# A norm's factors spread by two products of rounded parts, in place of one product in fp32

## The chip, the cores and the metric

The kernel runs on one core of a Trainium2 chip. The metric is the device time of one execution in microseconds, lower is better. A profiled execution gives, beside its own time, a trace of every instruction on TensorE (PE, with its weight loads listed apart as PEld), VectorE (DVE), ScalarE (ACT), GpSimd (POOL) and SyncE (SP, which only issues transfers here).

## What is computed

A decoder trunk of two layers on 512 tokens of 1024 features. Layer 0 mixes by a causal convolution module, layer 1 by differential attention; each is followed by a SwiGLU feed-forward and a gated embedding. Ahead of each of these parts stands a norm over the features of a token:

```
def rms_norm(x, g):
    xf = x.astype(jnp.float32)
    y = xf * lax.rsqrt(jnp.mean(xf * xf, axis=-1, keepdims=True) + EPS)
    return (y * g.astype(jnp.float32)).astype(x.dtype)

for i in range(DEPTH):                       # DEPTH = 2
    u = rms_norm(h, mixer_norm_g)
    h = h + (conformer_conv(u) if i % 2 == 0 else diff_attention(u))
    u = rms_norm(h, ffn_norm_g[i])
    h = h + swiglu(u, ffn_w_gate[i], ffn_w_up[i], ffn_w_down[i])
    gate = jax.nn.sigmoid(rms_norm(h, ple_norm_g[i]) @ ple_w_gate[i])
    h = h + gate * (p[i] @ ple_w_proj[i])
```

There are six such norms; five of them (all but that ahead of attention) need the factor of a token, the rsqrt, as a row that lies on all 128 partitions.

## The kernel before

**Layout.** The activations lie transposed: eight tiles `h[c]` of 128 features by 512 tokens. A linear layer multiplies weight tiles (128 by 128, stationary) with 512 tokens (moving) and sums over eight feature chunks in PSUM.

**Products in three parts.** Operands are split into a rounded part in the type F32R and the rest, also F32R: `hi` is an ACT copy, `lo = x - hi` a DVE subtraction (for weights lines 159 and 161 in `weight`). `mm3` (lines 164 to 168) adds three products, lo·hi, hi·hi and hi·lo. In the trace both types appear as "f32" on PE; the lines tell them apart. Products of operands that stay in plain fp32 (the sums of columns in line 199, transposes, and line 282 below) are single calls.

**Norms.** The linear layer takes `h * g` without the factor; the factor is multiplied in afterwards, on its result, since it is the same for all features of a token. The way to it:

- `chunk` (or `columns_of_chunks` for the first norm): ACT squares each `h[c]`, POOL adds the squares into `acc`.
- `columns_sum` (line 199): PE sums `acc` over the partitions, in four products of 128 by 128, so that token t of block b stands on partition t.
- `rsqrt_cols`: DVE scales and adds EPS (line 265, 128 by 4 values), POOL raises to -0.5 (line 267). The result `r` is 128 by 4.
- `diagonal` (line 272): DVE multiplies the identity, repeated four times, with `r`: a tile `dg` of 128 by 512 with the factors on four diagonals. It is taken from the four buffers `wk`.
- `spread` (line 282): PE multiplies a matrix of ones with `dg`: every partition of the PSUM tile `tp` then holds the row of 512 factors.
- `rows` (line 257): ACT copies that row to the tile `rb` in SBUF.
- DVE multiplies the accumulators by `rb`: line 514 in the convolution, lines 869 and 871 in the feed-forward, line 912 in the gated embedding.

**Where.** `diagonal` and `spread` are called for five norms: in the convolution's first chunk (lines 496 and 497), in the first pair of each feed-forward (lines 863 and 867) and in each gated embedding (lines 919 and 921). In program order the diagonal stands ahead of one more product of a full chunk (24 calls of 128 by 512), and the spread behind it. The layer norm inside the convolution (lines 575 to 589) builds a diagonal of its own with ACT.

**Order.** The Tile framework's planner writes the order of each engine's instructions: each is given a priority by its place in the program, and the planner, with modelled costs, lets each engine take the first by priority that is ready in its model. On the chip each engine then runs its list in order, so that an instruction that has to wait holds all that stands behind it on the same engine. Some places are tied by hand (`issue_after`, and one stretch with `manual_schedule`). The buffers come from rings under a tag: `wk` has four, `tp` two (PSUM), `mm` four (PSUM), `r8` and `v8` two each.

**Convolution stage.** The eight chunks of the convolution's first layer have their taps run in part on DVE (line 449), in part on ACT and POOL (lines 436, 437), and for four chunks (`PHASED`) on PE (line 398), with a hop through DRAM (`pi`, lines 361 to 367) that lays the tokens out anew; a second hop (`po`) brings the result back.

Of the kernel before, what the change touches and what calls it, by code (L numbers as in the profile page):

```python
# [13 lines left out]
F32R = mybir.dt.float32r  # L14
AF = mybir.ActivationFunctionType
ALU = mybir.AluOpType
# [4 lines left out]
P = 128  # L21
# [70 lines left out]
def trunk(ctx, tc, xT, pT, wts, diag, dww, vec, rel, onehot, lamv, out):  # L92
    nc = tc.nc
    V, A, G, T = nc.vector, nc.scalar, nc.gpsimd, nc.tensor
# [7 lines left out]
    def sb(shape, tag, bufs, dt=F32):  # L102
        uid[0] += 1
        return pool.tile(shape, dt, tag=tag, name=f"{tag}_{uid[0]}", bufs=bufs)
# [8 lines left out]
    wk = lambda dt=F32, shape=(P, S): sb(list(shape), "wk", 4, dt)  # L113
    big = lambda dt=F32, shape=(P, S): sb(list(shape), "big", 5, dt)
    f = lambda ap: ap.bitcast(F32)
# [10 lines left out]
    ident = sb([P, P], "ident", 1)  # L126
    make_identity(nc, ident)
    ones_r = sb([P, P], "ones", 1, F32R)
    ones = f(ones_r)
# [4 lines left out]
    t = wk()[:, 0:P]  # L134
# [4 lines left out]
    t = tp()  # L139
# [69 lines left out]
    class Norm:  # L209
# [41 lines left out]
        def diagonal(self):  # L251
            self.dg = diagonal(self.columns())

        def rows(self):

            r = sb([P, S], "rb", 1)
            A.copy(r, spread(self.dg))
            return r
# [4 lines left out]
    def rsqrt_cols(src, n, inv):  # L263
        v = sb([P, P // 2], "v8", 2)[:, :8]
        last_v[0] = V.tensor_scalar(v[:, :n], src, inv, EPS, ALU.mult, ALU.add)
        r = sb([P, P // 2], "r8", 2)[:, :8]
        last_pow[0] = G.tensor_tensor(r[:, :n], v[:, :n], mhalf[:, :n], ALU.pow)
        return r[:, :n]

    def diagonal(r):  # L270
        dg = wk()
        V.tensor_tensor(
            dg.rearrange("p (b t) -> p b t", b=4),
            ident.unsqueeze(1).to_broadcast([P, 4, P]),
            r.unsqueeze(2).to_broadcast([P, 4, P]),
            ALU.mult,
        )
        return dg

    def spread(dg):  # L280
        t = tp()
        T.matmul(t, ones, dg, start=True, stop=True)
        return t


# [205 lines left out]
    for c in range(NC):  # L491
        wa, wg = pairs[c]
        if c == 0:
            pg = half(wg)
            pa = half(wa)
            norm.dg = diagonal(norm.columns_of_chunks(3))
            rb = norm.rows()
# [81 lines left out]
    r = rsqrt_cols(vs[:, 0:4], 4, 1.0)  # L579
# [4 lines left out]
    dg = wk()  # L584
# [360 lines left out]
    rl = sb([33, NH], "big", 5)  # L945
# [6 lines left out]
    for k in range(2):  # L952
        t = tp()
# [447 lines left out]
```

## Time and profile before

| | before |
|---|---|
| median of 3 runs | 1249.58 us (1247.31 to 1250.39) |
| the profiled execution | 1249.66 us |
| its span, first to last instruction | 1247.6 us |
| granted clock of TensorE | 0.999 |
| ACT busy | 623.0 us (50%) |
| POOL busy | 470.5 us (38%) |
| HBM | 108 GB/s over the span |

How to read the views. A page of the profile gives each engine's busy time and its share of the span. PE's matmuls are pipelined: a matmul of 512 columns is listed with some 0.39 us while the next starts 0.23 us after it, so a busy PE may still be waiting in part; distances between starts, and the chain of waits, say more. The chain of waits is followed back from the last instruction, at each step to what released it, or to the instruction ahead of it on its engine. In the timeline a row gives start and duration in us, engine, line, operation and operands, a count where equal rows were merged, and in brackets the engine's idle time before and what ended it. In the list of waits stand the total, the number and the longest.

### The profile page before, as it was taken

The numbers are of one execution on the slowest core, as the hardware profiler recorded it, in microseconds if no ns is written. First come the engines' busy times: TensorE is split into PE (matmuls) and PEld (weight loads), VectorE is DVE, ScalarE is ACT, GpSimd is POOL, SyncE is SP. The second block draws the span as 40 slices with busy tenths as digits, with TensorE's granted clock in tenths as the row PEclk, the third lists the DMA queues.
The fourth block names the chain that finished last, engine by engine and source line by source line (L and its number), as shares of the span: only waits on it lengthen the run. The fifth ranks groups of instructions, "written<-read, shape, count | busy, mean of one in ns | idle before, by whom it ended". The sixth has DMA issues, their size and how long they took to land.

```text
span 1247.6 us, 18420 instructions
## 1 busy us (share of the span) xinstructions
PE 1236.4 (99%) x7080; PEld 1081.5 (87%) x7080; DVE 877.6 (70%) x1230; ACT 623.0 (50%) x1096; POOL 470.5 (38%) x355
## 2 busy tenths in 40 slices
PE   9999999999999999999999999999999999999998
PEld 7888788888998899888888888788889998999887
DVE  6998866985895478546676876646966885588535
ACT  5653464533553255334666877735434552455432
POOL 3763442024670365132346635041026640562220
PEclk9999999999999999999999999999999999999999
DMA  7566214324233322334432331142333333233321
GB/s 267 175 205 206 82 51 121 96 97 127 85 102 118 102 87 76 109 104 143 122 119 75 113 92 36 51 147 88 92 118 97 102 117 108 82 102 88 104 97 67
DMA packets 49154, 136.33 MB, mean 109 GB/s; under 512 B 5635, under 2 KB 10243, under 8 KB 49068
## 3 DMA queue, kind: packets, MB, share of 16 engines
q1 hardware_dynamic: 46944, 131.74, 33.7%
q10 hardware_dynamic: 2124, 3.43, 1.0%
q8 instruction: 55, 0.90, 0.3%
q14 instruction: 31, 0.25, 0.1%
HBM read 128.84 MB, written 6.31 MB: 108 GB/s over the span
## 4 chain that ended last, share of the span: by engine, by line
PE 88%; DVE 5%; issue 2%; DMA 1%; ACT 1%; SPq 0%; POOL 0%; DVEq 0%; ACTq 0%
PE mm L166 27%; PE mm L167 27%; PE mm L168 27%; PE mm L1117 1%; DVE sc L449 1%; DVE wlo L161 1%; PE sc L1085 1%; PE sc L1084 1%; PE tp L1104 1%; PE sc L398 1%; PE mm L398 1%; PE tp L1038 1%; PE mm L354 1%; PE tp L199 1%; DVE wlo L711 0%
## 5 line engine op out<-in xcount | busy, mean ns | idle before, releaser
L159 ACT CAST whi<-wraw 128x1024 fp32r<-128x1024 f32 (+2 forms) x145 | 145.6, 1013 | 220.2 <-PE mm L168 97.2
L161 DVE TENSOR_TENSOR wlo<-wraw,whi 128x1024 fp32r<-128x1024 f32 (+2 forms) x141 | 179.3, 1277 | 73.7 <-ACT whi L159 73.5
L166 PE MATMUL mm<-A,wlo 128*128 128x512 f32 (+1 forms) x568 | 222.5, 392 | 0.3 <-ACT A L206 0.2
L167 PE MATMUL mm<-A,whi 128*128 128x512 f32 (+1 forms) x568 | 219.8, 388 | 0.0
L168 PE MATMUL mm<-A,whi 128*128 128x512 f32 (+1 forms) x568 | 217.6, 389 | 0.0
L166 PE MATMUL mm<-B,wlo 128*128 128x512 f32 x352 | 137.9, 392 | 0.0
L167 PE MATMUL mm<-B,whi 128*128 128x512 f32 x352 | 137.8, 391 | 0.0
L168 PE MATMUL mm<-B,whi 128*128 128x512 f32 x352 | 136.2, 391 | 0.0
L229 POOL TENSOR_TENSOR acc<-acc,wk 128x512 f32<-128x512 f32 x35 | 58.3, 1665 | 194.5 <-ACT wk L228 193.9
L166 PEld LDWEIGHTS mm<-A,wlo 128*128 128x128 f32 x568 | 106.9, 188 | 23.6 <-issue 1.4
L167 PE MATMUL mm<-C,whi 128*128 128x256 f32 x448 | 127.0, 283 | 0.0
L168 PE MATMUL mm<-C,whi 128*128 128x256 f32 x448 | 127.0, 283 | 0.0
L166 PE MATMUL mm<-C,wlo 128*128 128x256 f32 x448 | 127.0, 283 | 0.0
L167 PEld LDWEIGHTS mm<-A,whi 128*128 128x128 f32 x568 | 107.0, 188 | 22.0 <-issue 1.0
L168 PEld LDWEIGHTS mm<-A,whi 128*128 128x128 f32 x568 | 106.6, 188 | 21.9 <-issue 0.5
L711 DVE TENSOR_TENSOR wlo<-A,whi 128x1024 fp32r<-128x1024 f32 x60 | 104.6, 1752 | 21.0 <-ACT whi L710 21.0
L710 ACT CAST whi<-A 128x1024 fp32r<-128x1024 f32 x60 | 62.9, 1048 | 56.6 <-PE mm L168 45.3
L720 POOL TENSOR_TENSOR A<-wraw 128x512 f32<-128x512 f32 x16 | 25.4, 1589 | 170.3 <-DMA wraw<-in_wts 156.1
L720 POOL TENSOR_TENSOR A<-A 128x512 f32<-128x512 f32 x16 | 25.3, 1581 | 161.9 <-DMA A<-in_wts 159.2
L167 PEld LDWEIGHTS mm<-C,whi 128*128 128x128 f32 x448 | 86.1, 192 | 0.2
L166 PEld LDWEIGHTS mm<-C,wlo 128*128 128x128 f32 x448 | 86.1, 192 | 0.2
L168 PEld LDWEIGHTS mm<-C,whi 128*128 128x128 f32 x448 | 86.1, 192 | 0.0
(309 smaller groups left out, 3030.6 us busy)
## 6 DMA issues: line engine op xcount, KB each, us to landing
wraw<-in_wts SPq DMA_DIRECT2D x161, 512.0 KB, 3.6
A<-in_wts SPq DMA_DIRECT2D x32, 512.0 KB, 3.6
wraw<-in_wts SPq DMA_DIRECT2D x16, 384.0 KB, 3.1
D<-in_diag SPq DMA_DIRECT2D x22, 256.0 KB, 4.7
C<-in_diag SPq DMA_DIRECT2D x16, 256.0 KB, 4.4
h<-in_xT SPq DMA_DIRECT2D x8, 256.0 KB, 5.2
rest<-h SPq DMA_DIRECT2D x8, 256.0 KB, 2.5
bias<-scr ACTq DMA_DIRECT2D x8, 256.0 KB, 3.7
```

The lines of the kernel that those rows point to most:

```text
L159: A.copy(hi[:, cut], raw[:, cut])
L161: eng.tensor_tensor(lo[:, cut], raw[:, cut], f(hi[:, cut]), ALU.subtract)
L166: T.matmul(acc, al, bh, start=first, stop=False, **kw)
L167: T.matmul(acc, ah, bh, start=False, stop=False, **kw)
L168: return T.matmul(acc, ah, bl, start=False, stop=last, **kw)
L199: r = T.matmul(t[:, cut], src[:, cut], ones, start=first and b == 0, stop=last and b == 3)
L229: self.last = self.eng.tensor_tensor(self.acc, self.acc, sq, ALU.add)
L354: last_tap[0] = T.matmul(acc, dg[:, j % 4], ups[c][:, j : j + S], start=(j == 0), stop=(j == PE_TAPS[c] - 1))
L398: last_tap[0] = T.matmul(acc[:, g * P : (g + 1) * P], w, ups[c][:, g, LEAD - m : LEAD - m + P], start=(m == 0), stop=(m == LAGS - 1),)
L710: A.copy(hi, src)
L711: V.tensor_tensor(lo, src, f(hi), ALU.subtract)
L720: G.tensor_tensor(s[:, 0], r1[:, 0], r1[:, 1], ALU.add)
```

## The change

`diagonal` splits `r` into a rounded part `rh` (a DVE copy into F32R) and the rest `rl` (a DVE subtraction), both 128 by 4, and multiplies the identity with each: two tiles of 128 by 512 in F32R, both from `wk`. `spread` adds two products with the ones in F32R in the same PSUM tile. The small tiles come from the rings `r8` and `v8`, which `rsqrt_cols` uses too. Nothing else in the program is touched.

```
     def diagonal(r):
-        dg = wk()
-        V.tensor_tensor(
-            dg.rearrange("p (b t) -> p b t", b=4),
-            ident.unsqueeze(1).to_broadcast([P, 4, P]),
-            r.unsqueeze(2).to_broadcast([P, 4, P]),
-            ALU.mult,
-        )
+        rh = sb([P, P // 2], "r8", 2, F32R)[:, :4]
+        rl = sb([P, P // 2], "v8", 2)[:, :4]
+        V.tensor_copy(rh, r)
+        V.tensor_tensor(rl, r, f(rh), ALU.subtract)
+        dg = wk(F32R), wk(F32R)
+        for d, part in zip(dg, (f(rh), rl)):
+            V.tensor_tensor(
+                d.rearrange("p (b t) -> p b t", b=4),
+                ident.unsqueeze(1).to_broadcast([P, 4, P]),
+                part.unsqueeze(2).to_broadcast([P, 4, P]),
+                ALU.mult,
+            )
         return dg
 
     def spread(dg):
         t = tp()
-        T.matmul(t, ones, dg, start=True, stop=True)
+        for i, d in enumerate(dg):
+            T.matmul(t, ones_r, d, start=i == 0, stop=i == 1)
         return t
```

## The prediction, made before the changed kernel was run

> **What bounds the kernel now.** First the engines' busy times and the chain by engine, on the page:
>
> ```profile
> PE 1236.4 (99%) x7080; PEld 1081.5 (87%) x7080; DVE 877.6 (70%) x1230; ACT 623.0 (50%) x1096; POOL 470.5 (38%) x355
> ...
> PE 88%; DVE 5%; issue 2%; DMA 1%; ACT 1%; SPq 0%; POOL 0%; DVEq 0%; ACTq 0%
> ```
>
> PE sets the time: it is 88% of the chain that ended last. A busy share alone would not show that, since a listed matmul outlasts the start of the next. Next the list of PE's waits over the whole span, nine rows of which the first three and the last stand here:
>
> ```profile
> PE tp L141 <- POOL ident masks.py:199: 1.5, 1, 1.5
> PE sc L398 <- DMA C<-pi: 1.3, 1, 1.3
> PE sc L1084 <- DVE st L1087: 1.3, 2, 1.0
> ...
> PE mm L166 <- ACT A L206: 0.2, 1, 0.2
> ```
>
> The nine come to 6.5 us (1.5, 1.3, 1.3, 0.7, 0.6, 0.4, 0.3, 0.2, 0.2), and none is for `rb`, for a diagonal or for a split weight `wlo`. So PE time saved is time won, except ahead of a wait, where it becomes more waiting.
>
> Then the five spreads and their users, by line:
>
> ```profile
> L282 PE MATMUL tp<-wk,ones x10: 590/590/592, 27.8 to 1214.3; 128*128 128x512 f32 x10
> ...
>   ACT rb L257: 17.2, 4
> ```
>
> Ten records for five calls: an fp32 product runs as two passes. ACT waits for four of the spreads, 17.2 us in all, 4.3 us each. The chain, read at those places, holds the spread at four of five, and one ordinary product beside it shows the usual price:
>
> ```profile
> 218.58 0.23 PE mm L168
> 218.81 0.86 PE tp L282 x2
> 568.40 0.86 PE tp L282 x2
> 864.66 0.86 PE tp L282 x2
> 1214.04 0.86 PE tp L282 x2
> ```
>
> The fifth, at 27.8 us, is not on the chain, which begins behind it, at 33.55 us, on DVE. PE's timeline at the second spread says the same by starts:
>
> ```profile
> 218.42 0.39 PE L168 MATMUL mm<-A,whi 128*128 128x512 f32 x1
> 218.65 1.02 PE L282 MATMUL tp<-wk,ones 128*128 128x512 f32 x2
> 219.10 0.80 PE L166 MATMUL mm<-A,wlo 128*128 128x512 f32 x1
> 219.74 0.40 PE L167 MATMUL mm<-A,whi 128*128 128x512 f32 x1
> ```
>
> From 218.65 to 219.74 are 1.09 us for the spread and one L166; less 0.23 for that one, the spread holds PE for 0.86.
>
> **PE's part.** The new spread is two products of F32R operands, 512 columns each, into one PSUM tile. The rows for that form are those of `mm3`, 0.23 us from start to start, each with its own weight load. Removed 0.86, added 2 x 0.23 = 0.46: 0.40 saved per spread. From both sides: if the two products ran at the old pass's 0.43 each, nothing would be saved; nothing in the rows is cheaper than 0.23, so 0.40 is the most. I take 0.40, as every L166 to L168 is of this type and shape.
>
> [...]
>
> **DVE's part.** Per norm a copy and a subtraction of 128 by 4 and a second product of 128 by 512 are added:
>
> ```profile
> L272 DVE TENSOR_TENSOR wk<-ident,r x5: 684/692/694, 22.7 to 1208.8; 128x512 f32<-128x512 f32 x5
> ...
> L999 DVE COPY rcol<-r x1: 170/170/170, 615.6 to 615.6; 128x4 f32<-128x4 f32 x1
> ...
> L577 DVE TENSOR_TENSOR v<-v x1: 164/164/164, 150.5 to 150.5; 128x4 f32<-128x4 f32 x1
> ```
>
> 0.17 + 0.16 + 0.69 = 1.02 us later for the last half of the diagonal, in all 5.1 us of DVE work. Is it in PE's way? Spread 2 starts at 218.65, and its diagonal is this one; the split that stands behind it on DVE:
>
> ```profile
> 213.59 0.68 DVE L272 TENSOR_TENSOR wk<-ident,r 128x512 f32<-128x512 f32 x1
> ...
> 215.66 1.23 DVE L161 TENSOR_TENSOR wlo<-wraw,whi 128x1024 fp32r<-128x1024 f32 x1 [1.39 <-ACT whi L159]
> ```
>
> The diagonal would be ready at 213.59 + 0.68 + 1.02 = 215.29, still 3.4 before PE takes it. The split behind it waited 1.39 for ACT, so 1.02 fits in. Spread 4 has the same pattern. Spreads 3 and 5:
>
> ```profile
> 563.22 0.69 DVE L272 TENSOR_TENSOR wk<-ident,r 128x512 f32<-128x512 f32 x1 [1.20 <-POOL r L267]
> ...
> 564.81 1.23 DVE L161 TENSOR_TENSOR wlo<-wraw,whi 128x1024 fp32r<-128x1024 f32 x1 [0.90 <-ACT whi L159]
> 568.25 1.02 PE L282 MATMUL tp<-wk,ones 128*128 128x512 f32 x2
> ```
>
> The diagonal is ready at 564.93, 3.3 before PE's turn; the split starts 0.1 late (1.02 against 0.90). PE waits for no `wlo` anywhere, so this costs nothing; were that cover gone, it would be 0.1. If the planner put the second product behind the split as well, it would end at about 564.93 + 1.23 = 566.2, still 2 us early. The new wait (the copy on POOL's power) is the old one, and the same instructions stand behind it. The second `wk` buffer costs nothing: `acc` is complete before `r` exists, so no square holds a buffer then, and the next taker comes after the spread; without that a square would wait some 4 us, off the chain. `r8` and `v8` are asked for again much later. No DMA moves, and POOL's and SP's work stays.
>
> **The first spread** is different, since DVE leads the convolution stage. The window of 36 to 107 us, and the rows around the first spread:
>
> ```profile
> 36.00:107.00 71.00, 69.69 (x378) 59.53 (x376) 68.72 (x79) 37.08 (x52) 49.79 (x36) 1.00 0.59 182
> ```
>
> ```profile
> 22.66 0.69 DVE L272 TENSOR_TENSOR wk<-ident,r 128x512 f32<-128x512 f32 x1 [1.14 <-POOL r L267]
> ...
> 24.83 1.22 DVE L161 TENSOR_TENSOR wlo<-wraw,whi 128x1024 fp32r<-128x1024 f32 x1 [1.48 <-ACT whi L159]
> ...
> 29.79 0.69 DVE L514 TENSOR_TENSOR big<-mm,rb 128x512 f32<-128x512 f32 x1 [1.63 <-ACT rb L257]
> ...
> 30.86 0.62 ACT L304 CAST wtl<-wraw 128x512 fp32r<-128x512 f32 x1 [1.10 <-DMA wraw<-in_pT]
> ...
> 31.50 1.28 ACT L515 ACT_TABLE_LOAD   x1
> ...
> 32.80 1.34 ACT L515 ACTIVATE big<-big,vec 128x512 f32<-128x512 f32 x2
> 33.55 0.75 DVE L532 SCALAR_TENSOR_TENSOR C<-big,vec,big 128x512 f32<-128x512 f32 x1 [1.88 <-ACT big L515]
> ```
>
> DVE is busy for 68.72 of 71 us there (the third busy time, behind PE and PEld), but not yet at 24 us: 1.02 fits into the 1.48 that it waits for ACT. The row `rb` would come 0.40 sooner and L514 with it, but the sigmoid stands on ACT behind a cast that a transfer releases at 30.86, so L532, with which the chain begins, stays. PE is 0.40 ahead and gives it back at its wait of 1.3 for the hop `pi` at 107 us: that wait becomes 1.7. Gain here 0, at most 0.40.
>
> **Sum.** 4 x 0.40 + 0 = 1.60 us off the profiled execution's 1249.66 (its span of 1247.6 and 2.06 around it): 1248.06, so **1248.1**, down 0.13%. The median before, 1249.58, is 0.08 below that execution, which changes nothing. About 0.3% (3.75 us: under 1245.8 or over 1253.3) is what a measurement of this kernel can tell from no change, so the forecast is "no difference".
>
> **Rivals.** (a) PE gains nothing: the F32R products with the ones take 0.43 each, or PE was not the bound. For it: PEld is at 87%, not 99%. Against: the distances of 0.23 on both sides of the spread and PE's 6.5 us of waits. The time would be 1249.7. [...]
>
> (b) The planner, with other costs for two engines, writes another order, and a better one. The chain around the wait for the hop:
>
> ```profile
> 97.85 1.14 DVE big L524
> 99.00 2.11 DVE wlo L161
> ...
> 101.12 0.33 SPq L155
> ...
> 102.93 3.77 DMA C<-pi
> ```
>
> SP issues the hop behind a weight load that waits for DVE's splits. With the hop ahead of them it could go up to 2.11 + 0.33 = 2.44 us sooner; PE has only 1.3 to win, and the first spread's 0.40 then counts: 1248.06 - 1.7 = 1246.4. The end of this road is all of PE's 6.5 us and all five spreads: 1249.66 - 2.0 - 6.5 = 1241.2.
>
> (c) Slower: the other order is a worse one. PE already waits for that hop, so any microsecond that DVE or SP is late with it is PE's. The place is this stage (DVE 68.72 of 71 us); the price is 1.02 if the first diagonal's extra work pushes DVE's list, and 2.44 for each of the hops that comes to stand behind one more pair of splits. With 1.02 and two such, 1248.06 + 1.02 + 4.88 = 1254.0. It decides from the point where DVE's 1.02 no longer fits into the 1.48 at 24 us, or where two instructions change places on DVE's or SP's list. Against: nothing that the planner sees changes by more than about 1 us, and the spread's turn on PE comes 3.3 us after its operand.
>
> (d) The diagonal comes after PE's turn and the spread, and `rb` with it, a slot later. It would need 3.3 us and has 1.02 against it; I give it no chance of its own beyond (c).
>
> **Chances.** Forecast (1248.1) 0.48; (a) 0.08; (b) 0.20, of which 0.14 under 1245.8; (c) 0.24, of which 0.18 over 1253.3, since a list of thousands of instructions that a planner orders anew has more worse neighbours than better ones when PE waits only 6.5 us of 1247.6. So faster 0.14, within 0.3% 0.68, slower 0.18. The range takes in forecast, (a), and of (b) and (c) the nearer parts: 1244.5 to 1253.0; the unknown costs (0 to 0.40 per spread, 0 to 0.40 for the first, 1.02 of DVE) lie inside. About 0.2 is left out.
>
> **What would show it.** PE: in the chain the spread at 0.46 x2 in place of 0.86, starting at most some 0.4 us sooner per spread before it. DVE: L272's successor twice per norm at 0.69, copy and subtraction at 0.16 to 0.17, and the next L161's idle time shrunk by about 1. ACT's wait for the row before L257 nearly unchanged, above 3.5 us. At 107 us the wait for the hop near 1.7. I am wrong if a spread is no longer behind the last product of its pair, if PE waits for a diagonal or `rb`'s users, or if the stages between the spreads (convolution 36 to 150, attention 600 to 830) change length by over 0.5 us: then it is the planner's order, not the costs counted here.

## The result, and the profile after

The changed kernel takes 1251.19 us (median of 22 runs, 1249.36 to 1252.74), the kernel before 1249.49 us (22 runs, 1247.31 to 1251.93). The ratio is 1.0013 with a 95% interval of 1.0007 to 1.0018: **slower by 0.13%**, some 1.7 us, where 1.6 us less were forecast. The profiled execution took 1251.76 us, its span was 1250.0 us.

What was forecast of the operations themselves is there. The rows of the new spread by line, and the three DVE operations by line (duration least, median, most):

```profile
L288 PE MATMUL tp<-wk,ones x10: 389/389/389, 28.9 to 1217.6; 128*128 128x512 f32 x10
```

```profile
L273 DVE CAST r<-r x5: 162/170/171, 23.6 to 1211.6; 128x4 fp32r<-128x4 f32 x5
```

```profile
L274 DVE TENSOR_TENSOR v<-r,r x5: 161/161/164, 23.8 to 1211.8; 128x4 f32<-128x4 f32 x5
```

```profile
L277 DVE TENSOR_TENSOR wk<-ident,r x5: 684/684/686, 23.9 to 1211.9; 128x512 fp32r<-128x512 f32 x5
L277 DVE TENSOR_TENSOR wk<-ident,v x5: 684/684/686, 24.5 to 1212.5; 128x512 fp32r<-128x512 f32 x5
```

Ten products of 0.39 us in place of ten of 0.59, and 0.17 + 0.16 + 0.68 of added DVE work per norm. PE's timeline at the second spread of the changed kernel (start, duration):

```profile
222.43 0.39 PE L167 MATMUL mm<-A,whi 128*128 128x512 f32 x1
222.66 0.39 PE L288 MATMUL tp<-wk,ones 128*128 128x512 f32 x1
222.88 0.39 PE L168 MATMUL mm<-A,whi 128*128 128x512 f32 x1
223.11 0.39 PE L288 MATMUL tp<-wk,ones 128*128 128x512 f32 x1
223.34 0.39 PE L166 MATMUL mm<-A,wlo 128*128 128x512 f32 x1
```

Every start is 0.23 us behind the one before: a spread costs 0.46, as forecast. So the loss lies elsewhere. PE's waits, the first four rows of the changed kernel (total, number, longest):

```profile
PE sc L404 <- DMA C<-pi: 3.2, 1, 3.2
PE tp L141 <- POOL ident masks.py:199: 1.5, 1, 1.5
PE sc L1090 <- DVE st L1093: 1.3, 2, 1.0
PE mm L166 <- DVE big L774: 1.0, 3, 0.5
```

L404 is line 398 of the kernel before, the taps that PE runs for a phased chunk: the wait for the hop through DRAM has grown from 1.3 to 3.2 us. What follows the wait is the second finding. The same 36 taps, first before, then after:

```profile
107.22 4.26 PE L398 MATMUL sc<-C,D 128*128 128x128 f32 x36 [1.29 <-DMA C<-pi]
```

```profile
109.42 5.88 PE L404 MATMUL sc<-C,D 128*128 128x128 f32 x36 [3.25 <-DMA C<-pi]
```

They take 5.88 in place of 4.26 us, 1.62 more, though nothing of them was changed. The granted clock, the third figure from the end in the table by stretch, is 0.53 and 0.62 there in place of 1.00. One row of the kernel before, then three of the changed kernel:

```profile
110.00:112.00 2.00, 2.00 (x21) 2.00 (x20) 2.00 (x4) 0.48 (x1) 1.54 (x2) 1.00 0.70 203
```

```profile
110.00:112.00 2.00, 2.00 (x12) 2.00 (x12) 1.97 (x3) 1.17 (x2) 1.12 (x1) 0.53 0.32 123
112.00:114.00 2.00, 2.00 (x13) 2.00 (x13) 2.00 (x4) 0.40 (x1) 1.38 (x2) 0.62 0.41 123
114.00:118.00 4.00, 4.00 (x38) 4.00 (x37) 3.89 (x6) 0.00 (x0) 0.00 (x0) 1.00 0.59 177
```

The hop is 2.20 us later, and the taps end 3.8 us later. The starts of the same instructions in both traces show where PE stands. At 103 us the changed kernel is level with the kernel before (0.02 us behind). At the start of the layer norm's sums it is 3.58 us behind (147.08 against 150.66 us), and from there it wins back at the four later spreads: 3.56 behind at 211 us, 3.16 at 560, 2.70 at 612, 2.64 at 857, 2.18 at 900, then 2.86 at 1205 and 2.41 at the end. Each of the four gives 0.45 or 0.46 across the spread itself; 0.7 is lost again at 1000 to 1022 us, where the changed kernel's PE waits 0.6 for DVE (line 774) and the kernel before's does not wait. The whole loss ahead of the layer norm is made between 103 and 120 us.

The loss of clock is not in every execution. Three of the 22 have a mean granted clock of 1.000 and took 1249.4 to 1249.5 us, the median of the kernel before; the four with 0.997 took 1251.6 to 1252.7 us.

Where the hop's delay begins is seen on ACT. The rows of the changed kernel's timeline around the first spread, ACT and DVE:

```profile
29.57 0.62 ACT L310 CAST wth<-wraw 128x512 fp32r<-128x512 f32 x1 [2.23 <-DMA wraw<-in_pT]
...
31.16 0.62 ACT L310 CAST wtl<-wraw 128x512 fp32r<-128x512 f32 x1 [0.97 <-DMA wraw<-in_pT]
...
31.69 0.58 ACT L257 COPY rb<-tp 128x512 f32<-128x512 f32 x1
...
32.30 0.69 DVE L520 TENSOR_TENSOR big<-mm,rb 128x512 f32<-128x512 f32 x1 [3.70 <-ACT rb L257]
...
34.34 0.76 DVE L538 SCALAR_TENSOR_TENSOR C<-big,vec,big 128x512 f32<-128x512 f32 x1 [0.15 <-ACT big L521]
```

The two lists of ACT differ here by one exchange: before, the copy of the row `rb` stood between the casts of `wth` and `wtl`; now it stands behind the cast of `wtl`, which waits for a transfer. The row is there at 31.69 in place of 29.18, DVE's first use of it at 32.30 in place of 29.79, and DVE's chain starts at 34.34 in place of 33.55. Part of these delays is not the change's: this execution is 0.91 us late on PE already at 12 us, ahead of anything that was changed. From there the lists of DVE, ACT, POOL and SP differ in many places up to 130 us.

The chain of waits ahead of the hop, after:

```profile
98.40 1.87 DVE big L530
...
100.27 2.10 DVE wlo L161
...
102.39 0.33 SPq L155
...
102.81 0.38 SPq L417
...
103.25 0.42 SPq L417
...
103.77 0.38 SPq L371
...
105.14 4.04 DMA C<-pi
```

Against before, DVE's operand of the hop is ready 1.28 us later (100.27 against 98.99), its own duration 1.87 in place of 1.14. The split behind it is the same one (2.10 and 2.11 us). Then SP has two loads of `po` (line 417) ahead of the hop; in the kernel before it has one:

```profile
101.54 0.38 SPq L411
...
102.02 0.38 SPq L365
```

### The profile page after: what moved, and what is told of

The parts are those of the page before. It is cut to its first block, busy times and chain, and to the rows that moved or that the text cites. A ratio compares the mean times of both kernels' runs of the same rounds, so it can differ in the third digit from the quotient of the medians.

```text
span 1250.0 us, 18431 instructions
## 1 busy us (share of the span) xinstructions
PE 1236.1 (99%) x7080; PEld 1083.2 (87%) x7080; DVE 883.6 (71%) x1245; ACT 623.7 (50%) x1096; POOL 470.2 (38%) x355
## 4 chain that ended last, share of the span: by engine, by line
PE 88%; DVE 3%; issue 1%; ACT 1%; DMA 1%; SPq 0%; POOL 0%; DVEq 0%; ACTq 0%
PE mm L166 27%; PE mm L167 27%; PE mm L168 27%; PE mm L1123 1%; PE sc L404 1%; PE sc L1091 1%; PE sc L1090 1%; DVE sc L455 1%; PE tp L1110 1%; PE mm L404 1%; DVE wlo L161 1%; PE tp L1044 1%; PE mm L360 1%; PE tp L199 1%; DVE wlo L717 0%
## 5 line engine op out<-in xcount | busy, mean ns | idle before, releaser
L726 POOL TENSOR_TENSOR A<-wraw 128x512 f32<-128x512 f32 x16 | 24.7, 1542 | 169.4 <-DMA wraw<-in_wts 116.2
```

Of the source, the lines that this page charges most:

```text
L726: G.tensor_tensor(s[:, 0], r1[:, 0], r1[:, 1], ALU.add)
```

## The experiments

**The theory** after this comparison (A): the convolution's first norm alone makes the loss. Its diagonal is ready 1 us later in the planner's model; the planner then writes another order in the convolution stage, the hop comes late, PE waits over 3 us (3.25) and the granted clock behind it is lower (0.53 from 110 to 112 us). **The rivals**: each of the five norms costs a little (B), the F32R products save nothing (D), DVE's added work itself delays the stage that DVE leads (E).

**Only the first norm changed.** `diagonal` gets a flag for the old form, and only the call in the convolution takes the new one:

```
-    def diagonal(r):
+    def diagonal(r, two=False):
+        if not two:
+            dg = wk()
...
+            return dg
...
-            norm.dg = diagonal(norm.columns_of_chunks(3))
+            norm.dg = diagonal(norm.columns_of_chunks(3), True)
```

> Only the first norm's spread (convolution) is changed, the other four stay fp32. The lists of DVE, ACT, POOL, SP and PE in the convolution stage are then those of the changed kernel. Theory A (the planner's other order in the convolution stage makes the hop of the fifth phased chunk late, PE waits some 3 us for it and runs at a lower granted clock for a few us behind): slower than before by about 3.3 us, so 1252.8, with the wait of 3.2 us before the phased taps and a granted clock well under 0.9 in the 4 us behind it. Rival B (each of the five norms costs a little, 5.1 us of DVE work spread over the kernel): a fifth of the measured loss of 1.7, so 1249.8. Rival C (no place; chance of one execution): 1249.5, no difference.

Measured 1252.56 us (1251.72 to 1252.75) against 1249.52 for before: ratio 1.0025 (1.0015 to 1.0036), slower by 3.0 us. The two places again, taps and clock by stretch:

```profile
109.36 5.88 PE L416 MATMUL sc<-C,D 128*128 128x128 f32 x36 [3.31 <-DMA C<-pi]
```

```profile
110.00:112.00 2.00, 2.00 (x11) 2.00 (x11) 1.96 (x3) 1.27 (x2) 1.23 (x2) 0.50 0.41 166
112.00:114.00 2.00, 2.00 (x16) 2.00 (x15) 2.00 (x4) 0.29 (x1) 1.27 (x2) 0.74 0.36 131
114.00:118.00 4.00, 4.00 (x39) 4.00 (x38) 3.89 (x6) 0.00 (x0) 0.00 (x0) 1.00 0.63 213
```

One norm of five costs more than all five together. Rival B is out, and so is C, no difference.

**The other four changed.** The same flag, the other way round (`two=True`, and `False` in the convolution).

> The first norm's spread stays fp32, the other four are changed. The order in the convolution stage is that of the kernel before. Theory A: faster than before by 4 x 0.40 = 1.6 us, so 1247.9. Rival B (every norm costs): slower by four fifths of 1.7, so 1250.9. Rival D (PE gains nothing by the F32R products): 1249.5.

Measured 1247.50 us (1246.30 to 1248.28): ratio 0.9984 (0.9976 to 0.9993), faster by 2.0 us. Rivals B and D are out; four spreads are worth what the sum gave them (1.6, inside the interval of 0.9 to 3.0). This version beats both kernels. With the run before it, +3.0 and -2.0 make +1.0 beside the +1.7 measured for the whole change.

**DVE's work without the order.** The old diagonal and the old spread stay; behind the first diagonal stand the three added DVE instructions, into a tile that nobody reads:

```
-            norm.dg = diagonal(norm.columns_of_chunks(3))
+            r = norm.columns_of_chunks(3)
+            norm.dg = diagonal(r)
...
+            V.tensor_copy(rh, r)
+            V.tensor_tensor(rl, r, f(rh), ALU.subtract)
+            V.tensor_tensor(
+                wk(F32R).rearrange("p (b t) -> p b t", b=4),
+                ident.unsqueeze(1).to_broadcast([P, 4, P]),
+                rl.unsqueeze(2).to_broadcast([P, 4, P]),
+                ALU.mult,
+            )
```

> The kernel before, with the copy, the subtraction and the second product of the first norm added on DVE behind the old diagonal, into a tile that nobody reads; the spread stays one fp32 product. The lists of all engines stay those of before but for these three instructions. Theory A: 1.02 us of DVE work fit into the idle 1.48 us at 24 us, no difference, 1249.5. Rival E (DVE leads this stage and its 1.02 us push everything behind): slower by 1.0, or by up to 2.6 if the longer wait lowers the granted clock.

Measured 1249.44 us (1248.73 to 1253.15): ratio 1.0006 (0.9997 to 1.0015; the ratio is taken over all executions and is not the quotient of the two medians). No difference that can be told. Rival E's 1.0 us would be 1.0008, which the interval still holds, but its loss of 2.6 or the 3.0 of the run with one norm lie outside; in the trace the taps behind the hop start at 107.30, against 107.22 before, with a wait of 0.9. Within these executions the clock shows: the eight with a mean granted clock of 0.999 or 1.0 lie at 1248.7 to 1250.1, the three with 0.998 at 1251.5 to 1253.2.

**The same work, with the order.** The three instructions ahead of the diagonal in place of behind it:

```
             r = norm.columns_of_chunks(3)
-            norm.dg = diagonal(r)
...
             V.tensor_copy(rh, r)
...
+            norm.dg = diagonal(r)
```

> As the run before in the sum of its work, but the three added DVE instructions stand ahead of the first norm's diagonal, so that it is ready 1.02 us later in the planner's model; with that alone the planner writes, in the convolution stage, nearly the order of the changed kernel (POOL's list the same, DVE's, ACT's and SP's with a few differences). The spread stays one fp32 product, so nothing is saved. Theory A: as slow as the first of these runs plus 0.4, slower than before by about 3.7, 1253.2, with the long wait ahead of the phased taps. Rival E (the work, not the order): the same as the run before it, whatever that gives.

Measured 1252.80 us (1251.77 to 1255.00): ratio 1.0032 (1.0019 to 1.0045), slower by 3.3 us between the medians. The sum of work is that of the run above; only the diagonal is later, and with it the lists are nearly those of the changed kernel. Its row is copied behind the cast as well:

```profile
30.62 0.62 ACT L304 CAST wtl<-wraw 128x512 fp32r<-128x512 f32 x1 [1.21 <-DMA wraw<-in_pT]
...
31.15 0.58 ACT L257 COPY rb<-tp 128x512 f32<-128x512 f32 x1
```

This pair shows that the order costs, not the work. Nor is it the later diagonal itself that holds anything on the chip: in this trace it is done at 24.7 us, and the spread starts at 29.3. DVE's chain starts as early as in the run above (33.80 and 33.81 us), and the hop is late all the same (taps from 108.99, with a wait of 2.9).

**PE's part of the first norm alone.** The old diagonal written in F32R, spread by two F32R products of the same tile, the second over the first (each has `start=True`); the rest of the factors is left out.

```
-    def spread(dg):
+    def spread(dg, ones=ones, n=1):
...
-        T.matmul(t, ones, dg, start=True, stop=True)
+        for _ in range(n):
+            T.matmul(t, ones, dg, start=True, stop=True)
...
-            norm.dg = diagonal(norm.columns_of_chunks(3))
-            rb = norm.rows()
+            norm.dg = diagonal(norm.columns_of_chunks(3), F32R)
+            rb = sb([P, S], "rb", 1)
+            A.copy(rb, spread(norm.dg, ones_r, 2))
```

> The kernel before, but the first norm's diagonal is written in F32R and spread by two F32R products of the same tile, the second over the first, so that the rest of the factors is left out; PE's saving of the first norm alone, without DVE's added work. The order of all lists stays that of before but for the spread. Theory: PE's 0.40 us are given back at the wait for the hop, so no difference, 1249.5, at most 0.4 less. Rival: the F32R products save nothing, or the saving counts in full: 1249.5 or 1249.1.

Measured 1249.34 us (1247.77 to 1250.74): ratio 1.0001 (0.9993 to 1.0010). The wait for the hop is 1.7 us in its list of waits, 0.4 more than before: the 0.40 is given back there, as the prediction had it.

**The one exchange undone.** The changed kernel, with the cast of `wtl` tied behind the copy of the first row:

```
-            A.copy(r, spread(self.dg))
+            self.copied = A.copy(r, spread(self.dg))
...
-            A.copy(hi, raw)
+            with tc.issue_after(norm.copied.ins) if layer == 0 and k == 1 else nullcontext():
+                A.copy(hi, raw)
```

> The changed kernel with one tie by hand: ACT's cast of the second feature tile (the one that fills wtl, which waits for a transfer) may only be issued behind the copy of the first norm's row. In the changed kernel the planner had put that copy behind the cast, 2.5 us later than before. Theory A1 (that one change of places starts the late order): the row is copied at about 29.5 us again, the hop's wait falls below 2.4 us, the granted clock behind it stays at 1.0, and the time is that of the kernel before less 4 or 5 savings of 0.4, 1247.5 to 1247.9. Rival A2 (the other changes of places on DVE's, SP's and ACT's lists count, whatever that copy does): it stays near 1251.

Measured 1249.71 us (1247.66 to 1251.94): ratio 1.0003 (0.9994 to 1.0012) to before. It lies between the two expectations. The row is copied at 29.04 and the hop arrives 2.0 us earlier than in the changed kernel (taps from 107.42 in place of 109.42), so the tie does what A1 says of the hop; but the clock fell all the same in the profiled execution:

```profile
107.42 5.88 PE L405 MATMUL sc<-C,D 128*128 128x128 f32 x36 [2.01 <-DMA C<-pi]
```

```profile
106.00:108.00 2.00, 0.57 (x3) 0.61 (x4) 0.55 (x2) 0.00 (x0) 0.00 (x0) 0.87 0.63 131
108.00:110.00 2.00, 2.00 (x11) 2.00 (x11) 1.96 (x3) 0.97 (x2) 0.86 (x1) 0.50 0.53 193
110.00:112.00 2.00, 2.00 (x16) 2.00 (x15) 2.00 (x4) 0.60 (x1) 1.65 (x2) 0.78 0.40 131
```

Its wait was 2.0 us, since PE was ahead. A1 is half right: the exchange makes the hop late, but undoing it does not always keep the clock. Of the eleven executions the six at 1247.7 to 1249.7 us have a mean granted clock of 0.999 or 1.000, and four of the five above them have 0.998.

**The second product on POOL.** In the first norm alone, the product with `rl` runs on POOL:

```
-    def diagonal(r):
+    def diagonal(r, low=V):
...
-        for d, part in zip(dg, (f(rh), rl)):
-            V.tensor_tensor(
+        for d, part, eng in zip(dg, (f(rh), rl), (V, low)):
+            eng.tensor_tensor(
...
-            norm.dg = diagonal(norm.columns_of_chunks(3))
+            norm.dg = diagonal(norm.columns_of_chunks(3), G)
```

> The changed kernel, but in the first norm alone the second diagonal product runs on POOL, which idles there, in place of DVE. The planner then leaves the row's copy ahead of the cast, and SP's and POOL's lists in the convolution stage are those of before, with a few changes of places on DVE's and one on ACT's. Theory A: all the savings and none of the loss, 1247.5 to 1247.9. Rival B (every norm's added work costs): near 1251, as the changed kernel.

Measured 1248.53 us (1246.70 to 1249.20): ratio 0.9992 (0.9983 to 1.0001). All five norms have the new form, and the loss is gone: the row stands ahead of the cast again (30.09 and 31.43 us), the wait for the hop is 1.0. The median's gain is smaller than expected. The interval, 1247.2 to 1249.5 us, holds both the expected 1247.5 to 1247.9 and no difference; the version with four norms remains the best seen.

**PE kept busy ahead of the hop.** The changed kernel with fifteen products that nobody reads (`last_mm3` holds the last product that `mm3` issued):

```
+            if c == 6:
+                fill = tp()
+                with tc.issue_after(last_mm3[0].ins):
+                    for _ in range(15):
+                        T.matmul(fill, ones_r, norm.u[7][0], start=True, stop=True)
             for k in BEHIND[c]:
                 pe_taps(k)
```

> The changed kernel with fifteen products of 128 by 512 that nobody reads on PE, behind the last product of the seventh chunk and ahead of the phased taps that wait for the hop; the planner moves five products of the next chunk from ahead of these taps to behind them. They fill 3.4 us of a wait that would be 3.2 + 1.1. Theory G (an idle PE of about 3 us makes the clock be granted less for some 3.5 us behind it, at a price of 1.6 us): the granted clock in the 8 us behind the start of the taps is 1.0 in every window, the taps run at their usual 0.11 us, and the time is 1251.2 - 1.6 + 1.1 = 1250.7. Rival (the slower taps have another reason, their operands): the taps stay slow, and the time is 1252.3.

Measured 1251.82 us (1249.62 to 1252.80): ratio 1.0020 (1.0009 to 1.0030). PE's timeline:

```profile
104.13 3.56 PE L524 MATMUL tp<-A,ones 128*128 128x512 f32 x15
108.62 4.26 PE L407 MATMUL sc<-C,D 128*128 128x128 f32 x36 [0.94 <-DMA C<-pi]
```

The taps are back at 4.26 us behind a wait of 0.94, and the granted clock is 1.00 in every stretch from 104 to 120 us: this is what theory G expects of the taps, and their operands came by the same late hop. The time does not decide: the median misses the expected 1250.7, but the interval, 1250.5 to 1253.1 us, holds it and the rival's 1252.3 too. In the profiled execution PE stood 1.27 us ahead of the changed kernel at 129 us and lost 0.9 of it again by 158 us, where it waits 1.2 for ACT in the layer norm in place of 0.7; the median shows no gain over the changed kernel, and why not more of it stays was not settled.

## Why the prediction was wrong

**Right:** the price of a spread (0.86 to 0.46, 0.40 saved), the added DVE operations (1.02 forecast, 1.01 measured), the four later spreads (1.6 forecast, 2.0 measured with an interval of 0.9 to 3.0, and 0.45 or 0.46 at each by the starts in the two traces), the work on DVE hidden at 24 us, and the first spread's 0.40 given back at the hop.

**Wrong:** the step that sets rival (c) aside, "nothing that the planner sees changes by more than about 1 us, and the spread's turn on PE comes 3.3 us after its operand", and with it the term for the first spread, "Gain here 0, at most 0.40". It measured +3.0 us. That the measured 1251.2 us lies inside the stated range is no merit of the forecast: the range reaches up there only for rival (c), and the forecast itself had the time fall. Two mistakes lie in that step.

First, the 3.3 us are slack on the chip and not in the planner's model. PE's list of the kernel before shows it, had it been read: each of the five spreads stands in the midst of a later accumulation, not behind the product that precedes it in the program. Directly behind the last product of its pair, where the prediction looked for it, no spread stood. The first (names shortened, with buffer numbers; `mm_316` is an accumulator of the second chunk):

```
L166 MATMUL mm_316<-A_22_124,wlo_252 128x512
L167 MATMUL mm_316<-A_22_124,whi_251 128x512
L282 MATMUL tp_241<-wk_238,ones_70 128x512
L168 MATMUL mm_316<-A_22_124,whi_251 128x512
```

An instruction with an earlier priority than its neighbours stands there only because the planner held it to be not ready sooner. So in the model each diagonal came just in time, and 1.02 us more moved every spread: in the changed list of PE the first product of each stands one or two places later, the second three. This is read from the lists and the planner's rule; the times of its model are not on record. At four places that cost nothing. At the first, the copy of the row lost its place ahead of a cast that waits for a transfer, and the stage that DVE leads went on in another order.

Second, the price of a late hop was taken as the wait alone. Of the 3.58 us lost by the layer norm, 1.96 are the longer wait (3.25 against 1.29) and 1.62 the slower taps behind it. The rest nets out: this execution began 0.91 later ahead of anything changed, and two savings of 0.44 make that up by 103 us (the first spread, and an fp32 product of the convolution, line 470, for which PE waited in its old place and does not in its new one); a product of 0.23 that now stands ahead of the taps no longer stands behind them.

The split of one trace has an error of its own, since the hop varies with the order unchanged. In the four traces whose order is that of the kernel before, but for the instructions added or replaced, the taps start at 107.2, 107.3, 107.7 and 108.3 us; in the four with the changed kernel's order, the late one, at 108.6, 109.0, 109.4 and 109.4. The size of the loss is therefore taken from the medians, +3.0 us.

The mechanism of rival (c), another order and a late hop, was the right one, its place too. Its chance of 0.24 was too small. Its prices were not those seen: neither 1.02 for DVE's work nor 2.44 for one more pair of splits ahead of the hop, but 0.73 for a DVE operation that takes longer in the new order, one more load of `po`, and 1.62 for the clock, which it did not name.

What stays open: which of the exchanges on DVE's and SP's lists make the remaining part of the hop's delay, since the tied version has other exchanges too.

## What to carry to other kernels

Where a planner writes the order, its slack is not the chip's: look in an engine's list for instructions that stand in the midst of work of later priority; they were placed the moment their operand was ready in the model, and a microsecond more moves them and what follows. A change of equal work should be tried at each of its places by itself, since one place can cost more than all others win: here four of five won 2.0 us and the fifth lost 3.0. And a wait on PE can cost more than its length: here the granted clock was 0.50 for 3.41 us behind the changed kernel's wait of 3.25 us, and the 36 taps took 1.62 us longer; in the kernel before it was 1.00 behind the wait of 1.29.

## What the runs showed of the hardware

In the profiled execution of the changed kernel the granted clock was 0.50 for 3.41 us, from 110.12 to 113.54 us, behind PE's wait of 3.25 us. At 0.50 these lose an estimated 1.7 us of PE's work; the taps took 1.62 us more. Not every wait was followed by this. The version with four norms waited 2.2 us and kept its clock; its taps and its stretch, beside those shown above:

```profile
108.31 4.25 PE L416 MATMUL sc<-C,D 128*128 128x128 f32 x36 [2.21 <-DMA C<-pi]
```

```profile
110.00:112.00 2.00, 2.00 (x21) 2.00 (x20) 1.97 (x4) 1.53 (x2) 1.93 (x2) 1.00 0.49 167
```

PE ran 21 matmuls in those two us where the changed kernel ran 12 at 0.53. The ten profiled executions, with the wait for the hop from the list of PE's waits and the lowest mean granted clock of a stretch of 2 or 4 us from 106 to 116 us:

| version | wait for the hop, us | lowest mean granted clock |
|---|---|---|
| only the first norm | 3.3 | 0.50 |
| the changed kernel | 3.2 | 0.53 |
| the same work, with the order | 2.9 | 0.50 |
| the other four changed | 2.2 | 1.00 |
| the one exchange undone | 2.0 | 0.50 |
| PE's part of the first norm alone | 1.7 | 1.00 |
| the kernel before | 1.3 | 1.00 |
| the second product on POOL | 1.0 | 1.00 |
| DVE's work without the order | 0.9 | 1.00 |
| PE kept busy ahead of the hop | 0.9 | 1.00 |

The wait of 2.0 us was followed by 0.50 and that of 2.2 us by 1.00, so the length of the wait alone does not order these. What does was not shown.

The DVE operation ahead of the hop (line 524 of the kernel before, 530 of the changed one, writing 128 by 128 by 4) stands beside an addition on POOL. First before, then after:

```profile
97.85 1.14 DVE L524 SCALAR_TENSOR_TENSOR big<-big,vec,big 128x512 f32<-128x512 f32 x1
...
97.99 2.02 POOL L482 TENSOR_TENSOR B<-B,wk 128x512 f32<-128x512 f32 x1
```

```profile
98.01 1.29 POOL L488 TENSOR_TENSOR B<-B,wk 128x512 f32<-128x512 f32 x1
...
98.40 1.87 DVE L530 SCALAR_TENSOR_TENSOR big<-big,vec,big 128x512 f32<-128x512 f32 x1
```

Before, DVE's operation starts first and takes 1.14 us, and POOL's takes 2.02; after, POOL's starts first and takes 1.29, and DVE's takes 1.87, 0.73 more. No run varied this alone, so the cause is not shown. A split also took 1.33 us in the kernel before (at 85.80 us) and 2.33 in the changed one (at 86.13); the cause of that is not shown either.
